# The input gate of the mLSTM branch as seven half-size products, query and key split for two token tiles at once, and a newly searched order

## The chip, the cores and the metric

The kernel runs on one core of a Trainium2 chip. The metric is the device time of one execution in microseconds; the kernel before took 1318.66 us (median of three runs, 1317.69 to 1319.36).

## The reference

Two layers of a decoder trunk, 512 tokens of width 1024, all in float32. One projection feeds two branches (differential attention and an mLSTM); the branches are gated, projected, merged by two sigmoid gates that are themselves slices of the projection, and projected again. Only the parts that matter here:

```python
def hybrid_layer(x, ...):
    h = rmsnorm(x, norm_g)
    proj = h @ w_in                                   # 512 x 1024 @ 1024 x 10256
    aq, ak, av, az, bqk, bv, bi, bf, bo, bz, ga, gb = jnp.split(proj, idx, axis=-1)
    q = rope(rmsnorm(two_map_heads(aq), q_norm_g), cos, sin)
    k = rope(rmsnorm(two_map_heads(ak), k_norm_g), cos, sin)
    ...
    ya = oa @ w_out_a                                 # attention branch
    ...
    yb = hb @ w_out_b                                 # mLSTM branch
    u = jax.nn.sigmoid(ga) * ya + jax.nn.sigmoid(gb) * yb
    return x + u @ w_o
```

`gb` is the gate on the mLSTM branch: `h` (512 x 1024) times a 1024 x 1024 slice of `w_in`.

## The kernel before

**Precision.** The matmuls take their operands as float32r. Each operand is split into a high part (a rounded copy, made by ScalarE) and a low part (the remainder, made by VectorE): `wh`, `wl` for weights, `hh`, `hl` for the normalised input. A product is three matmuls, high x high, high x low and low x high (`mm3`, L526).

**Pieces.** The projections are a list of pieces in the order of `TUNE["order"]`. Each piece brings one 128 x 1024 block of weights (512 KB), usually loaded by the SP queue into `wr` (two buffers), and split into `wh` and `wl`. Blocks named in `TUNE["dlo"]` are loaded by the POOL queue instead (`dh`), and their low part is formed by a copy and an accumulating load (`dl`). A feature piece (`feat_piece`: az, bqk, bo, bz, ga, gb, woa, wob; eight pieces each) makes 128 output features of all 512 tokens: 8 blocks of the inner dimension x 3 = 24 matmuls of 128 x 512 (128 columns of weights, 512 tokens moving). So `gb` costs 8 x 24 = 192 such matmuls in a layer. The gate's tanh goes to a small pool (`sgb`), and `wob_done` multiplies it in.

**Seven products.** `bv` and `wo` are not computed as eight half-size block products but as seven (`seven`, L904): left operand, right operand and output are each cut in 2 x 2 blocks, and sums of blocks are multiplied instead of blocks. The products are P1 to P7, each of two pieces. P1, P2 and P3 use weight blocks as they are; P5, P6 and P4 use a running sum `wws`, P7 a sum `wwt`. These sums are built by accumulating loads on the POOL queue or, for the steps in `TUNE["tdve"]`, by adds on VectorE (`load_sums` L1778, `prep_sums` L1794). The left operands P5, P6, P7 and P3 need are sums of blocks of `h`, called S1, S2, S3, S4 (`late_forms` L786), each a high and a low tile (`lhS`, `llS`). The products are summed in two PSUM chains of two tiles, X and Y, and one Z (`CHAIN`, L121).

**Queries and keys.** When a 128-token tile of a query-key column group has its norm and rotation, `qk_split` (L1077) transposes it on TensorE (four 128 x 128 transposes into one PSUM tile `qkt`), and ScalarE and VectorE split it into `qs`, `ks` and `kl`: per tile six copies and four subtractions on 64 partitions x 256 elements. `qkn` counts finished tiles; the attention scores of a head wait for them.

**Order.** All instructions are recorded first (`Recorder`, L128) and then put in order by a list scheduler with a table of costs and of biases (`schedule`, L298). Each engine then runs its instructions strictly in that order. Buffers come from pools; the largest, `qkp`, has 24 slots of 128 x 1024, shared by inputs, head outputs, operand sums, weight sums and `dh`/`dl`. A load that takes over a slot waits until the last reader of the slot's earlier tile is done, and what is queued behind it on SP or POOL waits too.

## Time and profile before

| what | value |
|---|---|
| median of 3 runs | 1318.66 us |
| the profiled execution's own time | 1318.76 us |
| its span on the page | 1317.0 us |
| VectorE busy | 1047.3 us (80%) |
| ScalarE busy | 941.6 us (71%) |
| GpSimd busy | 81.0 us (6%) |
| DMA, mean over the span | 128 GB/s |
| read from and written to HBM | 162.66 MB, 4.26 MB |

TensorE's rows are in the prediction. Each TensorE instruction has two rows in the profile, the weight load (PEld) and the matmul (PE). A matmul's recorded duration (some 390 ns at 128 x 512) is longer than the distance between two starts, since they are pipelined; what a matmul costs in a stream is the distance of the starts. "Busy" is the time covered by any record, so that what remains is idle time.

### The profile page before, as it was taken

To read this page: it belongs to the slowest core of one execution; us is meant where nothing else is said; L and a number is where in the kernel's file an instruction comes from. 1 tells how busy PE (TensorE), PEld (TensorE's weight loads), DVE (VectorE), ACT (ScalarE), POOL (GpSimd) and SP (SyncE) were. 2 spreads that over 40 slices of the span, in tenths; PEclk is the share of its full clock that TensorE was granted. 3 is DMA by queue.
4 is the path that set the end of the run, shared out by engine and by line. 5 is a ranking of instruction groups with operands and counts; after the bars stand their busy time and mean duration, and the time that the engine had idled before them with its cause. 6 is when DMAs were issued, how large, how long until landed. Compare 5 with 4: busy or idle time off the path is not lost.

```text
span 1317.0 us, 17544 instructions
## 1 busy us (share of the span) xinstructions
PE 1308.5 (99%) x6140; PEld 1084.6 (82%) x6140; DVE 1047.3 (80%) x1876; ACT 941.6 (71%) x1808; POOL 81.0 (6%) x104
## 2 busy tenths in 40 slices
PE   8999999999999999999999999999999999999998
PEld 6888888888888888888887888888888888888887
DVE  7899888897588788755887988888876788887466
ACT  6878789895367788743668787898944677887333
POOL 1000000000010000001101000000000101000000
PEclk9999999999999999999999999999999999999999
DMA  5222232233675465455954222322346655653656
GB/s 190 88 66 81 97 98 63 81 96 116 186 175 143 132 177 135 121 138 117 302 144 120 58 81 78 100 80 80 90 129 187 168 143 159 158 112 121 163 132 200
DMA packets 56744, 168.06 MB, mean 128 GB/s; under 512 B 6704, under 2 KB 13488, under 8 KB 56656
## 3 DMA queue, kind: packets, MB, share of 16 engines
q1 hardware_dynamic: 45712, 127.10, 30.7%
q0 software_dynamic: 10944, 39.85, 14.3%
q8 instruction: 48, 0.79, 0.2%
q14 instruction: 40, 0.33, 0.1%
HBM read 162.66 MB, written 4.26 MB: 127 GB/s over the span
## 4 chain that ended last, share of the span: by engine, by line
PE 96%; DVE 1%; DMA 1%; ACT 1%; issue 0%; SPq 0%; DVEq 0%; ACTq 0%
PE qk L474 13%; PE av L474 7%; PE az L474 7%; PE bo L474 7%; PE ga L474 7%; PE bqk L474 7%; PE bz L474 7%; PE woa L474 7%; PE gb L474 7%; PE wob L474 7%; PE wo_P L474 6%; PE bv_P L474 6%; PE sc L474 3%; PE num L474 2%; PE ms L474 2%; PE ut L474 1%
## 5 line engine op out<-in xcount | busy, mean ns | idle before, releaser
L474 ACT CAST wh<-wr 128x1024 fp32r<-128x1024 f32 x176 | 183.4, 1046 | 118.9 <-PE woa L474 27.9
L474 DVE TENSOR_TENSOR wl<-wr,wh 128x1024 fp32r<-128x1024 f32 (+1 forms) x178 | 212.6, 1196 | 54.3 <-ACT wh L474 53.0
L474 PE MATMUL qk<-wh,hh 128*128 128x512 f32 x240 | 88.6, 397 | 1.0 <-ACT hh L474 1.0
L474 PE MATMUL qk<-wl,hh 128*128 128x512 f32 x240 | 88.7, 399 | 0.3 <-DVE wl L474 0.3
L474 PE MATMUL qk<-wh,hl 128*128 128x512 f32 x240 | 87.3, 398 | 0.1
L473 ACT ACT_TABLE_LOAD x65 | 83.4, 1283 | 1.1
L474 ACT ACTIVATE p<-sc,mx,rq 128x128 f32<-128x128 f32 (+3 forms) x128 | 78.5, 618 | 6.3 <-DVE mx L474 5.5
L474 PE MATMUL woa<-oa,wh 128*128 128x512 f32 x224 | 71.7, 391 | 0.0
L474 PE MATMUL wob<-ob,wh 128*128 128x512 f32 x192 | 60.5, 389 | 0.0
L474 POOL DMA_DIRECT2D dl<-in_wp_dram x26 | 22.6, 871 | 532.7 <-ACT dl L474 406.3
L474 DVE TENSOR_REDUCE mx<-sc 128x2 f32<-128x256 f32 (+1 forms) x64 | 52.5, 820 | 0.8
L474 PEld LDWEIGHTS qk<-wh,hh 128*128 128x128 f32 x240 | 44.7, 188 | 9.8 <-ACT hh L474 1.3
L474 PEld LDWEIGHTS qk<-wl,hh 128*128 128x128 f32 x240 | 44.9, 188 | 9.5 <-DVE wl L474 0.9
L474 ACT CAST ks<-qkt 64x256 fp32r<-64x256 f32 x128 | 47.1, 368 | 7.4 <-DVE qs L474 5.7
L474 PEld LDWEIGHTS qk<-wh,hl 128*128 128x128 f32 x240 | 44.8, 188 | 8.9 <-DVE hl L474 0.4
L474 PEld LDWEIGHTS woa<-oa,wh 128*128 128x128 f32 x224 | 42.1, 188 | 8.7
L474 PE MATMUL az<-hl,wh 128*128 128x512 f32 x120 | 47.8, 399 | 0.0
L474 PE MATMUL az<-hh,wh 128*128 128x512 f32 x120 | 47.8, 399 | 0.0
L474 PE MATMUL az<-hh,wl 128*128 128x512 f32 x120 | 47.5, 397 | 0.0
L474 PE MATMUL av<-wl,hh 128*128 128x512 f32 x120 | 47.4, 395 | 0.0
L474 ACT CAST uh<-ut 128x128 fp32r<-128x128 f32 (+2 forms) x80 | 29.7, 372 | 24.7 <-PE ut L474 22.1
L474 PE MATMUL av<-wh,hl 128*128 128x512 f32 x120 | 47.2, 393 | 0.0
(378 smaller groups left out, 4013.1 us busy)
## 6 DMA issues: line engine op xcount, KB each, us to landing
wr<-in_wp_dram SPq DMA_DIRECT2D x174, 512.0 KB, 3.6
dh<-in_wp_dram POOLq DMA_DIRECT2D x26, 512.0 KB, 7.4
dl<-in_wp_dram POOLq DMA_DIRECT2D x26, 512.0 KB, 7.2
wws_wo<-in_wp_dram POOLq DMA_DIRECT2D x12, 512.0 KB, 5.9
dd<-rows SPq DMA_DIRECT2D x16, 256.0 KB, 4.9
wws_bv<-in_wp_dram POOLq DMA_DIRECT2D x8, 512.0 KB, 7.2
em<-rows SPq DMA_DIRECT2D x16, 256.0 KB, 6.8
dd<-rows SPq DMA_DIRECT2D x16, 192.0 KB, 5.4
```

The costliest lines, as they stand in the source:

```text
L473: self.tc.keep_in_program_order(self.nc.scalar.preload_act_table_set(self.SET_NAME[o["load"]]))
L474: self.tc.keep_in_program_order(getattr(o["e"], o["fn"])(*o["a"], **o["k"]))
```

## The change

Four things are changed together.

1. `gb` is made by `seven`, with the roles of the operands that the code calls FEAT7: weights are the stationary operand, half of the tokens (256) move. A product's piece has 4 feature blocks x 2 inner blocks x 3 = 24 matmuls of 128 x 256, so `gb` is 7 x 2 x 24 = 336 matmuls of 128 x 256 in a layer in place of 192 of 128 x 512. Its outputs (`gate_out`) are four tiles of the pool `s5`. S1 to S4 are formed once, for `bv`; because `gb` needs them again, `bv` writes them to DRAM (`h_spill`: eight 512 KB stores a layer) and `gb` reads them back (eight loads a layer).
2. `qk_split` waits for the second of two token tiles and works on both: two PSUM tiles (`qkt0` for queries, `qkt1` for keys), each of four transposes, and copies and subtractions of 64 x 512, half as many as before.
3. The scheduler's estimate of when a DMA lands is replaced (`land`), and some of its numbers are new.
4. `TUNE` is new: the order of the pieces, the biases, which norms are summed by a folded tile (`foldA`, `foldM`, `foldD`: folded, the sum over partitions takes one 128 x 512 matmul, unfolded two), which sums VectorE makes, and which blocks POOL loads.

The core of the diff:

```diff
 TUNE = {
     "order": (
-        ... bz6 bz7 gb3 wob3 gb4 gb2 wob2 wob4 gb0 gb5 wob0 wob5 gb1 gb6 wob1 gb7 wob6 wob7 wo.P5 ...
+        ... bo7 bo6 bz6 bz7 gb.P1 gb.P5 gb.P2 gb.P3 gb.P6 gb.P7 wob4 gb.P4 wob6 wob0 wob3 wob5 wob1 wob2 wob7 wo.P5 ...
     ),
-    "foldA": (1, 2, 3, 4, 5, 6, 7),
-    "foldM": (0, 1, 2, 3, 4, 5, 6, 7),
-    "foldD": (0, 1, 2, 3, 4, 5, 6, 7),
+    "foldA": (0, 2, 3, 4, 7),
+    "foldM": (1, 3, 4, 5),
+    "foldD": (0, 1, 2, 3, 4, 5, 6),
-    "tdve": {'bv': ('T2',), 'wo': ('T2', 'T3', 'T4')},
+    "tdve": {'bv': ('T1', 'T2', 'T4'), 'wo': ('T3',), 'gb': ('T2',)},
-    "lates": ('bv',),
+    "lates": ('bv', 'gb'),
...
         def qk_split(c, tt, rq):
-            def back():
-                pst = ps_tr.tile([P, 4, P], F32, tag="tr", name=f"qkt{l}_{c}_{tt}")
-                for g in range(4):
-                    T.transpose(pst[:, g, :], rq[:, g * P : (g + 1) * P], ident)
...
+            st[("rot", c, tt % 2)] = rq
+            if tt % 2 == 0:
+                return
+            rqs = [st[("rot", c, t)] for t in range(2)]
+            def back(side):
+                def f():
...
+                    pst = ps_tr.tile([P, 2, 2, P], F32, tag="tr", name=f"qkt{side}{l}_{c}_{tt}")
+                    for t in range(2):
+                        for g in range(2):
+                            T.transpose(pst[:, g, t, :], rqs[t][:, (2 * side + g) * P : (2 * side + g + 1) * P], ident)
...
+                    for r, (a, b) in enumerate(((L, H), (H, L))):
+                        t = st[("qs", c)][2 * side + r][:, :, ts]
+                        A.copy(t[a], src[a])
+                        if side:
+                            A.copy(t[b], src[a])
+                            t2_, o = st[("kl", c)][r][:, :, ts], a
+                        else:
+                            t2_, o = t, b
+                        V.tensor_tensor(t2_[o], src[a], t[a].bitcast(F32), ALU.subtract)
...
+            for side in range(2):
+                defer(TUNE["qkt"] + side, back(side))
```

How the order changes, at three places. In a row, the first number in a name is the layer; the tile written stands first, then what it is made from.

TensorE, layer 0, where `gb` begins before the change: a feature piece `gb0_3`, whose `wh87` and `wl87` are the high and low weights of one block, then `wob0_3`, and `gb0_4`.

```order
L474 MATMUL gb0_3_1011<-hh0_117,wl87_996 128x512
L474 MATMUL wob0_3_1029<-ob0_0_842,wh88_1003 128x512 x2
L474 MATMUL wob0_3_1029<-ob0_0_842,wl88_1004 128x512
L474 MATMUL wob0_3_1029<-ob0_1_866,wh88_1003 128x512 x2
L474 MATMUL wob0_3_1029<-ob0_1_866,wl88_1004 128x512
```

TensorE now, layer 0, inside `gb`: the tile `gb0_P5` is chain Y (for P5 and then P3), `gb0_P1` chain X (for P1, P6, P7, P4); `lhS20`/`llS20` and `lhS40`/`llS40` are the reloaded S2 and S4 of layer 0 (`lhS10`/`llS10`, S1, stand ahead); `num0_7` is the last mLSTM head.

```order
L498 MATMUL gb0_P5_0_1029<-lhS40_gb_1048,wh94_1056 128x256
L498 MATMUL gb0_P5_1_1030<-lhS40_gb_1048,wh94_1056 128x256
L498 MATMUL gb0_P5_0_1029<-llS40_gb_1049,wh94_1056 128x256
L498 MATMUL gb0_P5_1_1030<-llS40_gb_1049,wh94_1056 128x256
L498 MATMUL num0_7_1086<-sdl0_7_1046,bv0_1_0_767 128x512
L498 MATMUL gb0_P1_0_1021<-lhS20_gb_1060,wh95_1062 128x256
L498 MATMUL gb0_P1_1_1022<-lhS20_gb_1060,wh95_1062 128x256
```

The stretch of 128 x 512 matmuls, each on one block's weights, has become one of 128 x 256 with the reloaded sums as moving operand. The slot that `lhS20` is loaded into is that of `llS10`; between the last read of `llS10` and this first read of `lhS20` TensorE runs 53 matmuls, 44 of 128 x 256 and three each of 128 x 512, 128 x 384 and 128 x 128.

The SP queue, layer 0, at the end of the mLSTM heads, before: weight blocks `wr` and the last head's rows (`dd`, `em`).

```order
L474 DMA dd_7_1023<-rows 128x128
L474 DMA wr_1043<-in_wp_dram 128x1024
L474 DMA wr_1048<-in_wp_dram 128x1024
L474 DMA em_7_1024<-rows 128x512
L474 DMA wr_1053<-in_wp_dram 128x1024
```

The SP queue at the same place now:

```order
L498 DMA em_7_1001<-rows 128x512
L498 DMA lhS_gb<-dS1h_718 128x1024
L498 DMA llS_gb<-dS1l_719 128x1024
L498 DMA wwt_gb_1032<-in_wp_dram 128x1024
L498 DMA wr_1050<-in_wp_dram 128x1024
L498 DMA lhS_gb<-dS4h_729 128x1024
L498 DMA llS_gb<-dS4l_730 128x1024
L498 DMA wwt_gb_1051<-in_wp_dram 128x1024
L498 DMA wr_1055<-in_wp_dram 128x1024
L498 DMA lhS_gb<-dS2h_748 128x1024
L498 DMA llS_gb<-dS2l_749 128x1024
L498 DMA wr_1076<-in_wp_dram 128x1024
```

Between the weight blocks stand the reloads of S1, S4 and S2 and the first blocks of the sums; a weight block that is queued behind a reload waits for the reload's slot.

ScalarE, layer 0, where the second query-key group is split, before (`ks`, `qs` from the transposed tile `qkt0_1_0` of the first 128 tokens):

```order
L474 CAST ks00_1_280<-qkt0_1_0_314 64x2x128
L474 ACTIVATE sq0_1_3_300,qss0_1_2_298<-qk0_1_3_248 128x64 x4
L474 CAST qs10_1_279<-qkt0_1_0_314 64x2x128
L474 ACTIVATE qy0_1_3_302<-qss0_1_2_298,eps64_104 128x16
L474 ACTIVATE qy0_1_3_302<-qy0_1_3_302 128x16
```

ScalarE now (`qkt00_1_1` holds the queries and `qkt10_1_1` the keys of the first 256 tokens):

```order
L498 CAST qs10_1_279<-qkt00_1_1_319 64x2x256
L498 ACTIVATE qy0_1_3_301<-qy0_1_3_301 128x16
L498 CAST wh17_324<-wr17_321 128x1024
L498 ACTIVATE rot0_1_2_294<-rot0_1_2_294,rq0_1_284 128x64 x4
L498 CAST ks00_1_280<-qkt10_1_1_320 64x2x256 x2
```

The copies cover twice the tokens, and each stands once for two tiles.

More of the change, by code (lines that the diff above doesn't have):

```diff
@@ L37 @@
 TUNE = {
+    "land": (0.4, 300.0, 885.0, 2560.0, 3650.0),
     "order": (
[4 rows of a table removed]
[4 rows of a table added]
     ),
     "qkt": 5,
-    "gct": 15,
-    "gls": 1,
-    "glf": 0,
-    "attn": (0, 1, 6, 10, 10, 13, 15, 16, 19, 26),
+    "gct": 11,
+    "gls": 2,
+    "glf": 1,
+    "attn": (0, 8, 8, 12, 14, 14, 15, 16, 20, 27),
     "a0": 24,
     "ap": 18,
-    "a4": 18,
-    "ml": (6, 7, 12, 17, 19, 31),
+    "a4": 20,
+    "ml": (8, 8, 21, 21, 29, 41),
     "ahead": 3,
-    "lc": 4,
-    "slack": 2311.1,
+    "lc": 10,
+    "slack": 366.3,
     "margin": 0.0,
-    "pemargin": 117.1,
-    "wait": 228.9,
+    "pemargin": 141.5,
+    "wait": 162.2,
     "swpen": 141896579.9,
-    "smargin": 231.5,
+    "smargin": 781.4,
     "pwait": 0.0,
-    "wdiff": 7859.5,
+    "wdiff": 6612.9,
     "wsp": 4,
-    "kact": (0, 1, 2),
-    "qsq": (3,),
-    "foldA": (1, 2, 3, 4, 5, 6, 7),
-    "foldM": (0, 1, 2, 3, 4, 5, 6, 7),
-    "foldD": (0, 1, 2, 3, 4, 5, 6, 7),
+    "kact": (1, 2),
+    "qsq": (1, 3),
+    "foldA": (0, 2, 3, 4, 7),
+    "foldM": (1, 3, 4, 5),
+    "foldD": (0, 1, 2, 3, 4, 5, 6),
     "warm": 18,
@@ L72 @@
     "acl": 7,
-    "gateA": 6,
+    "gateA": 2,
     "gateM": 1,
-    "actp": (0, 1, 2, 3),
-    "m0": 224,
-    "mp": 18,
-    "m4": 8,
+    "actp": (2, 3),
+    "m0": 228,
+    "mp": 13,
+    "m4": 3,
     "slots": 24,
-    "hfd": 4,
+    "hfd": 20,
     "tset": (0, 18),
@@ L83 @@
     "pmask": 0,
-    "dlo": ('av0.3', 'az0', 'az6', 'bo1', 'bo4', 'bo6', 'bo7', 'bqk3', 'bz4', 'ga3', 'gb2', 'qk1.2', 'qk1.3', 'woa4', 'wob1', 'wob5'),
-    "dla": 5,
+    "dlo": ('av1.1', 'az0', 'az2', 'az3', 'az6', 'bo1', 'bo4', 'bo6', 'bo7', 'bqk3', 'bz3', 'ga3', 'ga5', 'gb0', 'gb1', 'qk0.3', 'qk1.2', 'qk2.0', 'woa0', 'woa4', 'woa6', 'wob1', 'wob5'),
+    "dla": 6,
     "groups": (),
@@ L92 @@
-    "drain": 105.8,
-    "group": 570.6,
-    "lates": ('bv',),
-    "risk": 118.2,
-    "late": 395.7,
[3 rows of a table added]
+    "drain": 137.0,
+    "group": 984.3,
+    "lates": ('bv', 'gb'),
+    "risk": 2827822086695.3,
+    "late": 10125509.6,
 }
@@ L291, in rate, with land @@
         if o["k"].get("accum_op") is not None:
-            return 150.0
-        return 175.0 if src.tensor.name.startswith("rows") else 250.0 if src.space != DRAM else 360.0
+            return 204.0
+        if o["eng"] == "POOL":
+            return 514.0
+        if src.space == DRAM and src.tensor.name.startswith("rows"):
+            return 138.0
+        return 316.0 if src.space == DRAM and math.prod(list(o["a"][0].shape)) >= 131072 else 310.0
+    def land(self, o, go, queue):
+        z = int(o["eng"] == "POOL")
+        size = 4.0
+        for x in list(o["a"][0].shape):
+            size *= x
+        w = size / self.rate(o)
+        share, g0, g1, f0, f1 = TUNE["land"]
+        own = 1.0 - share if z else share
+        t = max(go + (g1 if z else g0), queue[z])
+        r = queue[1 - z] - t
+        if r <= 0:
+            fin = t + w
+        elif w / own <= r / (1.0 - own):
+            d = w / own
+            fin = t + d
+            queue[1 - z] = fin + (r - d * (1.0 - own))
+        else:
+            d = r / (1.0 - own)
+            queue[1 - z] = t + d
+            fin = t + d + (w - d * own)
+        queue[z] = fin
+        return fin + (f1 if z else f0)
     LAT = {("ACT", "DVE"): 131, ("ACT", "PE"): 262, ("ACT", "ACT"): 153, ("DVE", "ACT"): 130, ("DVE", "PE"): 240, ("DVE", "DVE"): 127,
@@ L343, in schedule @@
         end = [0.0] * n
-        dma = 0.0
+        queue = [0.0, 0.0]
         table = 6
@@ L426, in schedule @@
             if o["fn"] == "dma_start":
-                size = 4.0
-                for x in list(o["a"][0].shape):
-                    size *= x
-                go = s + c if e == "POOL" else s
-                dma = max(dma, go) + size / self.rate(o)
-                end[i] = max(dma, go) + (5500.0 if e == "POOL" else 5000.0 if o["a"][1].tensor.name.startswith("rows") else 3000.0)
+                end[i] = self.land(o, s + c if e == "POOL" else s, queue)
             for t in o["tiles"]:
@@ L1003, in f @@
             def f():
-                if ("qd", c, tt) not in st or tt and st.get(("qkn", c), 0) < tt or not tt and not room(6):
+                if tt % 2 == 0:
+                    return
+                if ("qd", c, tt) not in st or tt > 1 and st.get(("qkn", c), 0) < tt - 1 or tt == 1 and not room(6):
                     return False
-                if not tt:
+                if tt == 1:
                     qk_take(c)
-                rq = t2(f"rl{l}_{c}_{tt}")
-                SY.dma_start(rq, st["qd", c, tt])
-                qk_split(c, tt, rq)
+                for t in (tt - 1, tt):
+                    rq = t2(f"rl{l}_{c}_{t}")
+                    SY.dma_start(rq, st["qd", c, t])
+                    qk_split(c, t, rq)
             return f
@@ L1058, in qk_done @@
             V.tensor_tensor(rqv, y, t, ALU.mult)
+            back = [st[("rot", c, t % 2)] for t in (tt - 1, tt)]
             for t in (tt - 1, tt):
-                qk_back(c, t, st[("rot", c, t % 2)])
+                qk_back(c, t, back[t % 2])
         def qk_back(c, tt, rq):
@@ L1095, in qk_split @@
-            defer(TUNE["qkt"], back)
+            st[("rot", c, tt % 2)] = rq
+            if tt % 2 == 0:
+                return
+            rqs = [st[("rot", c, t)] for t in range(2)]
+            def back(side):
+                def f():
+                    if side and ("qkq", c, tt) not in st:
+                        return False
+                    pst = ps_tr.tile([P, 2, 2, P], F32, tag="tr", name=f"qkt{side}{l}_{c}_{tt}")
+                    for t in range(2):
+                        for g in range(2):
+                            T.transpose(pst[:, g, t, :], rqs[t][:, (2 * side + g) * P : (2 * side + g + 1) * P], ident)
+                    ts = slice((tt - 1) * P, (tt + 1) * P)
+                    L, H = slice(0, 64), slice(64, 128)
+                    src = pst.rearrange("p g t k -> p g (t k)")
+                    for r, (a, b) in enumerate(((L, H), (H, L))):
[4 more added lines that the diff above has]
+                            t2_, o = st[("kl", c)][r][:, :, ts], a
+                        else:
+                            t2_, o = t, b
+                        V.tensor_tensor(t2_[o], src[a], t[a].bitcast(F32), ALU.subtract)
+                    if side:
+                        st[("qkn", c)] = tt + 1
+                    else:
+                        st["qkq", c, tt] = 1
+                return f
```

13 lines of the change are left out of this document (removed), and 10 rows, old and new, of the table TUNE.

## The prediction

> **What bounds the kernel now.** First the page's head, which has TensorE (PE) covered almost throughout, then the busy time by stages, which says where the rest lies, then the chain of waits.
>
> ```profile
> span 1317.0 us, 17544 instructions
> PE 1308.5 (99%) x6140; PEld 1084.6 (82%) x6140; DVE 1047.3 (80%) x1876; ACT 941.6 (71%) x1808; POOL 81.0 (6%) x104
> ```
>
> ```profile
> core 0: us, PE busy (x) PEld busy (x) DVE busy (x) ACT busy (x) POOL busy (x), PEclk, DMA share, GB/s
> 0.00:30.00 30.00, 26.58 (x120) 20.43 (x121) 22.49 (x70) 18.07 (x34) 4.95 (x9) 1.00 0.60 208
> 330.00:370.00 40.00, 40.00 (x178) 33.10 (x177) 25.20 (x27) 18.19 (x22) 4.31 (x5) 1.00 0.70 193
> ...
> 622.00:655.00 33.00, 33.00 (x147) 27.00 (x146) 29.20 (x38) 19.90 (x28) 4.19 (x5) 1.00 0.94 302
> 700.00:716.00 16.00, 14.99 (x74) 12.32 (x73) 12.43 (x27) 11.35 (x29) 0.00 (x0) 1.00 0.57 183
> ...
> 1290.00:1317.00 27.00, 22.95 (x101) 18.45 (x99) 17.11 (x21) 6.24 (x6) 1.73 (x2) 0.97 0.52 155
> ```
>
> PE is idle for 8.5 us. The first 30 us hold 3.42 of it (inputs on their way), the last 27 us 4.05 (the output leaving), 700 to 716 us 1.01: 8.48 together. Between start and tail there is one hole of 1 us, where a transpose waited for the split of the keys:
>
> ```profile
> PE ut L474 <- DVE kl L474: 1.0, 1, 1.0
> ```
>
> So the time is the sum of the distances between matmul starts, at a granted clock of 1.00. A new order can win back that hole and little else; what it can lose has no such bound. VectorE and ScalarE matter only where they make PE wait.
>
> What a matmul costs in a stream, by its width: in the chain of waits 45 of 128 x 512 in a row; in two stretches of the timeline of PE runs of four 128 x 256, with the start in the first column (the third row of each is what follows).
>
> ```profile
> 568.74 10.20 PE gb L474 x45
> ```
>
> ```profile
> 266.65 0.39 PE L474 MATMUL sc<-ks,qs 128*128 128x256 f32 x2
> 266.88 0.40 PE L474 MATMUL sc<-kl,qs 128*128 128x256 f32 x2
> 267.12 0.80 PE L474 MATMUL av<-uh,av 128*128 128x512 f32 x3
> ...
> 284.81 0.40 PE L474 MATMUL sc<-ks,qs 128*128 128x256 f32 x2
> 285.05 0.41 PE L474 MATMUL sc<-kl,qs 128*128 128x256 f32 x2
> 285.29 0.38 PE L474 MATMUL ut<-ct,p 128*128 128x128 f32 x2
> ```
>
> The wide one costs 10.20 / 45 = 226.7 ns; eight narrow ones took 0.47 + 0.48 us, 118.75 ns each. Two narrow ones cost 237.5 ns, 5% more than the wide one they replace. That eats part of what seven products save over eight.
>
> **The change part by part.**
>
> *The gate's matmuls.* The 2 x 192 that go stand in six groups of the trace, three like the first row and, for the blocks that POOL loads, three like the second:
>
> ```profile
> L474 PE MATMUL gb<-hh,wh 128*128 128x512 f32 x112 | 43.6, 390 | 0.0
> ...
> L474 PE MATMUL gb<-hl,dh 128*128 128x512 f32 x16 | 6.2, 390 | 0.0
> ```
>
> They are 3 x 112 + 3 x 16 = 384, at 226.7 ns 87.05 us. In come 2 x 336 = 672 of 128 x 256, at 118.75 ns 79.80 us. The trace has these only in runs of up to four, while the gate makes long streams. The nearest rows bound the price: half a wide one, 113.3 ns (76.2 us), below, and the dearer run, 120 ns (80.6 us), above. I take the mean of both runs, since a run's later starts are no further apart than its first. The break-even comes out of the sum below and lies close, at 124.8 ns.
>
> *The Trainium skill on this term.* By "TensorE: Matmul & The Clock Gate", section "Back-to-back issue gap", an isolated gap is N/2.4 + 2.5 ns, 109.2 and 215.8 ns; with these two the whole sum below would be an estimate of 6.5 us saved. The rows above have both widths some 10 ns higher, so the measurement decides.
>
> *Unfolded norms.* The new tables unfold 4 attention norms, 8 mLSTM norms and 2 denominators over both layers: 14 more matmuls of 128 x 512, 3.17 us on PE.
>
> *The sum on PE.* 87.05 - 79.80 - 3.17 = 4.08 us less; with the bounds 3.2 to 7.7 us. Transposes, scores and the other projections are as many as before, only moved.
>
> *Queries and keys in pairs.* ScalarE and VectorE, by these groups; the last two give the price of 64 x 512:
>
> ```profile
> L474 ACT CAST ks<-qkt 64x256 fp32r<-64x256 f32 x128 | 47.1, 368 | 7.4 <-DVE qs L474 5.7
> L474 ACT CAST qs<-qkt 64x256 fp32r<-64x256 f32 x64 | 23.4, 365 | 9.6 <-DVE kl L474 7.7 <-PE qkt L474 0.8
> L474 DVE TENSOR_TENSOR qs<-qkt,qs 64x256 fp32r<-64x256 f32 x64 | 27.0, 422 | 7.9 <-ACT qs L474 5.9
> L474 DVE TENSOR_TENSOR kl<-qkt,ks 64x256 fp32r<-64x256 f32 x64 | 26.8, 419 | 11.6 <-ACT ks L474 10.5
> L474 ACT CAST mk<-cv 64x512 fp32r<-64x512 f32 x16 | 9.7, 617 | 0.2
> L474 DVE TENSOR_TENSOR mk<-cv,mk 64x512 fp32r<-64x512 f32 x16 | 11.0, 686 | 1.3 <-ACT mk L474 0.9
> ```
>
> ScalarE goes from 70.5 to 96 x 0.617 = 59.2 us, VectorE from 53.8 to 64 x 0.686 = 43.9 us: 11 and 10 us less on engines that PE did not wait for, except in the 1 us hole. What the pairing costs is time until the first tile's scores may start. PE has other products queued then, so I put it at nothing; without that cover a hole like the old one costs 1 us. For the order as a whole I take nothing, between -1 us (hole closed) and +2 us (two such holes).
>
> *What the gate adds elsewhere.* VectorE gets eight weight sums of 128 x 1024 (four for `bv`, four for `gb`) and twelve adds of 128 x 512, over both layers about 8 x 1.2 + 12 x 0.69 = 18 us by this group and the last one above:
>
> ```profile
> L474 DVE TENSOR_TENSOR wl<-wr,wh 128x1024 fp32r<-128x1024 f32 (+1 forms) x178 | 212.6, 1196 | 54.3 <-ACT wh L474 53.0
> ```
>
> They lie beside PE, as does the split of a piece (1.2 us of VectorE in the 2.85 us of its 24 matmuls): from 622 to 655 us VectorE is busy for 29.20 of 33 us, and PE does not wait. Without that cover each sum would cost PE its 1.2 us. The DMAs are the point. In the gate's stage in after's order the SP queue issues 18 transfers of 512 KB (six weight blocks, four first blocks of sums, eight reloads of S1 to S4) and 1.8 MB of rows for two heads, the POOL queue eight of 512 KB. Their price by the queues' rows:
>
> ```profile
> q1 hardware_dynamic: 45712, 127.10, 30.7%
> q0 software_dynamic: 10944, 39.85, 14.3%
> ```
>
> The SP queue: 0.307 x 1317 / 127.10 = 3.18 us of all 16 engines a MB, 1.67 us for 512 KB (0.524 MB). POOL: 0.143 x 1317 / 39.85 = 4.73, 2.48 us. The stage needs 18 x 1.67 + 1.8 x 3.18 + 8 x 2.48 = 55.6 us of DMA. Its PE work is 344 x 0.11875 + 39 x 0.2267 = 49.7 us and 12 small matmuls below 0.2 us each: about 51 us. So DMA is full unless some 5 us or more of it is issued ahead of the stage, which the lookahead (two raw blocks, seven pieces for sums) allows. With the share at 0.94 between 622 and 655 us PE was busy for 33.00 of 33 us, and at 0.70 in `bv`, the seven-product stage that most resembles this one, for 40.00 of 40. I take no wait, and keep the other end as rivals. The eight stores of S1 to S4 fall into `bv`, which loses two weight-sum loads on SP and two on POOL a layer: up from 0.70 by (6 x 1.67 - 2 x 2.48) / 40 = 0.13, still below 0.94.
>
> *The forecast.* The profiled execution took 1318.76 us (span 1317.0), 0.1 us over the median of the runs shown. 1318.76 - 4.1 = **1314.7 us**.
>
> **The rivals.**
>
> *S2 comes late.* `lhS20` takes over a slot of S1. From the last read there to its first read PE runs 53 matmuls, 44 narrow ones (5.2 us), three wide (0.7 us) and six others (about 0.85): 6.7 us for issue and landing. The load's two prices, in the windows of `bv` and of 622 to 655 us:
>
> ```profile
> wr<-in_wp_dram SPq DMA_DIRECT2D x8, 512.0 KB, 3.6
> ```
>
> ```profile
> wr<-in_wp_dram SPq DMA_DIRECT2D x6, 512.0 KB, 8.5
> ```
>
> At 3.6 us it lands in time. At 8.5 plus about 0.6 to see the release and issue, PE waits 2.4 us; behind the waiting matmul stand the rest of P3 and all of P6, and behind the load on SP only what is read later (`wob4`'s block, S3's pair). That is 4.8 us in two layers, **1319.5 us**, no change. For: nearly full DMA engines. Against: S4's pair has 11 us and should have drained by then. 20%. Holes of the new order adding up to the same, 7%.
>
> *DMA binds the whole gate.* If nothing is issued ahead, the stage takes 55.6 / 0.94 = 59 us in place of 51: 8 us a layer, **1331 us**, slower. It turns slower from 3.4 us a layer. For: the sum above, and slots that come free late. Against: the 33.00 of 33 us at a share of 0.94. 10%.
>
> *Weight loads show.* A narrow matmul brings as many weights as a wide one. If a long stream were paced by the load's record of 0.19 us (its rows below, the timeline of PEld in the first stretch), 672 x (188 - 118.75) = 47 us would be added: **1361 us**.
>
> ```profile
> 266.77 0.30 PEld L474 LDWEIGHTS sc<-kl,qs 128*128 128x128 f32 x2
> 267.00 0.54 PEld L474 LDWEIGHTS av<-uh,av 128*128 128x128 f32 x3
> ```
>
> But two loads fit in 0.30 us, overlapping, and the starts stay 118 ns apart. 3%. The same page of the Trainium skill, section "Part 3: Packing small matmuls", says that weight loads overlap with running matmuls only when they target another row group; by that rule each of the 302 added matmuls would show its load. The trace does not agree: the loads here use all 128 rows and lie inside the distance of the starts.
>
> *It saves more.* Narrow matmuls at 113.3 ns or the hole closed: 1310 to 1312.5 us. 8%.
>
> **How the numbers follow.** Forecast 52%, more 8%, no change 27% (S2 20, holes 7), slower 13% (DMA 10, loads 3). A difference of 0.2%, 2.6 us, is about what a measurement of this kernel can tell from no change. Faster, below 1316.0: 0.60; same: 0.27; slower, above 1321.3: 0.13. The range takes in the saving's bounds and S2 coming late: 1310 to 1321 us, leaving out the 13%.
>
> **What would show it.** In the profile after: runs of `gb_P` matmuls with starts 118 to 120 ns apart (at 124.8 the saving is gone); PE busy without a hole over the gate's 51 us, and a DMA share there of 0.9 or more; no wait of `gb_P` on a DMA of `lhS` (S2's rival is an idle time of PE ahead of the first matmul that reads it); fewer and longer copies from `qkt`; idle time at start and tail as before. The forecast is wrong if the sum of PE's idle time grows by more than 2 us, or if a narrow matmul in a long stream costs another price than in a run of four.

## The result, and the profile after

The changed kernel is slower, not faster:

| kernel | median | lowest to highest | runs | ratio to before (95%) |
|---|---|---|---|---|
| before, beside it | 1318.61 us | 1317.69 to 1319.36 | 9 | |
| changed | 1325.23 us | 1321.33 to 1332.94 | 9 | 1.0062 (1.0047 to 1.0077) |

That is 6.6 us more, where the forecast had 4.0 less and the range ended at 1321. The second thing to see is the spread: 11.6 us, where the kernel before has 1.7. The profiled execution took 1332.73 us and is one of the longest of the nine, so a second profile was taken later (below); one profile of a kernel with such a spread is not its median. All medians leave out one execution, of e10, which took 1438.05 us at a granted clock (the share of TensorE's full clock that the profile shows as granted) of 0.851.

The head of the page, and TensorE's waits in that first profile (in total, times, longest):

```profile
span 1331.0 us, 18309 instructions
PE 1314.2 (99%) x6442; PEld 1101.2 (83%) x6442; DVE 1062.0 (80%) x1856; ACT 915.4 (69%) x1770; POOL 96.1 (7%) x124
```

```profile
PE gb_P L498 <- DMA llS_gb<-dS3l: 5.1, 2, 2.9
PE num L498 <- DVE ms_b L498: 2.2, 1, 2.2
```

PE is idle for 16.8 us, 8.3 more than before. The last line is a head of the mLSTM branch in layer 1, the first is the gate: once in each layer its product P7 waits for the low tile of S3, reloaded from DRAM. S2, which the prediction named as the rival, is not in the list. By stages, with start, `bv`, the gate in layer 0, 622 to 655 us and the gate in layer 1:

```profile
0.00:30.00 30.00, 26.15 (x107) 20.20 (x108) 19.60 (x50) 16.56 (x30) 4.64 (x9) 0.94 0.58 208
330.00:370.00 40.00, 40.00 (x178) 33.13 (x177) 23.77 (x23) 17.24 (x20) 1.73 (x2) 1.00 0.69 210
535.00:600.00 65.00, 62.74 (x434) 58.74 (x433) 45.56 (x59) 46.35 (x63) 8.02 (x10) 0.97 0.84 240
622.00:655.00 33.00, 32.58 (x143) 26.35 (x142) 30.94 (x46) 17.87 (x24) 4.08 (x5) 1.00 0.72 206
1190.00:1255.00 65.00, 62.15 (x430) 58.16 (x429) 46.98 (x61) 48.18 (x66) 8.02 (x10) 0.97 0.83 228
```

The gate loses 2.3 and 2.9 us to idle time, and its granted clock is 0.97, where it was 1.00. The hole between 700 and 716 us is gone (16.00 of 16 busy). In the second profile of the same kernel, of an execution of 1323.28 us, the wait on S3 stands first again:

```profile
PE gb_P L498 <- DMA llS_gb<-dS3l: 3.3, 2, 2.5
PE warm L498 <- DVE ml L498: 1.6, 1, 1.6
PE num L498 <- DVE ms_b L498: 1.0, 1, 1.0
```

(The `warm` line is the start, as before; `num` is another head here, in layer 0 at 526 us.) So the wait on S3 belongs to the kernel, not to one execution. Part of what separates 1332.7 from 1323.3 us shows in the clock behind it. After the wait in layer 0, in the first profile and in the second:

```profile
572.78 0.38 PE L498 MATMUL gb_P<-llS_gb,wh 128*128 128x256 f32 x1 [2.26 <-DMA llS_gb<-dS3l]
...
574.61 0.63 PE L498 MATMUL gb_P<-lhS_gb,wh 128*128 128x256 f32 x2
575.04 0.63 PE L498 MATMUL gb_P<-llS_gb,wh 128*128 128x256 f32 x2
575.47 0.63 PE L498 MATMUL gb_P<-lhS_gb,wl 128*128 128x256 f32 x2
```

```profile
572.45 0.39 PE L498 MATMUL gb_P<-llS_gb,wh 128*128 128x256 f32 x1 [2.48 <-DMA llS_gb<-dS3l]
...
573.87 0.40 PE L498 MATMUL gb_P<-lhS_gb,wh 128*128 128x256 f32 x2
574.11 0.40 PE L498 MATMUL gb_P<-llS_gb,wh 128*128 128x256 f32 x2
574.35 0.40 PE L498 MATMUL gb_P<-lhS_gb,wl 128*128 128x256 f32 x2
```

In the second the pairs start 0.24 us apart, 120 ns a matmul. In the first, from some 0.9 us behind the end of the wait, the matmuls are slow, and the pairs start 0.43 us apart, 214 ns each: the clock is at half, and the windows say so (from 574 to 577 us in the first, from 572 to 575 in the second):

```profile
574.00:577.00 3.00, 3.00 (x16) 3.00 (x16) 0.00 (x0) 0.00 (x0) 0.00 (x0) 0.50 1.08 416
```

```profile
572.00:575.00 3.00, 2.55 (x21) 2.55 (x22) 0.96 (x2) 0.40 (x1) 0.00 (x0) 1.00 1.10 385
```

PE is fully busy in the first and makes 16 matmuls; the second makes 21 in the same 3 us, with 0.45 us idle. Sixteen slow matmuls cost 16 x 94 ns = 1.5 us, which no list of waits shows. Both profiles have the same order of matmuls, so they can be set against each other start by start. Of the 9.5 us by which the first falls behind, 4.8 arise at the two waits on S3 with the slow matmuls behind them, 1.4 in the first 30 us (where the first profile also has 3.4 us at half clock), 1.2 at the two heads and 2.1 in `wo` of layer 0.

### The profile page after: what moved, and what is told of

The parts are those of the page before. It is cut to its first block, busy times and chain, and to the rows that moved or that the text cites. A ratio compares the mean times of both kernels' runs of the same rounds, so it can differ in the third digit from the quotient of the medians.

```text
span 1331.0 us, 18309 instructions
## 1 busy us (share of the span) xinstructions
PE 1314.2 (99%) x6442; PEld 1101.2 (83%) x6442; DVE 1062.0 (80%) x1856; ACT 915.4 (69%) x1770; POOL 96.1 (7%) x124
## 4 chain that ended last, share of the span: by engine, by line
PE 91%; DMA 5%; DVE 2%; ACT 1%; issue 1%; SPq 0%; DVEq 0%; ACTq 0%
PE qk L498 13%; PE av L498 9%; PE ga L498 7%; PE bo L498 7%; PE bqk L498 7%; PE woa L498 7%; PE wob L498 7%; PE az L498 6%; PE bz L498 6%; PE gb_P L498 5%; PE wo_P L498 4%; PE bv_P L498 4%; PE sc L498 3%; PE num L498 2%; DMA llS_gb<-dS3l 2%; PE ms L498 1%
## 5 line engine op out<-in xcount | busy, mean ns | idle before, releaser
L498 ACT CAST wh<-wr 128x1024 fp32r<-128x1024 f32 x166 | 172.4, 1043 | 115.1 <-DMA wr<-in_wp_dram 30.2
L498 DVE TENSOR_TENSOR wl<-wr,wh 128x1024 fp32r<-128x1024 f32 (+1 forms) x168 | 199.9, 1195 | 34.9 <-ACT wh L498 32.2
L498 PE MATMUL qk<-wl,hh 128*128 128x512 f32 x224 | 80.8, 397 | 0.4 <-DVE wl L498 0.4
L498 PE MATMUL qk<-wh,hh 128*128 128x512 f32 x224 | 79.4, 397 | 1.0 <-ACT wh L498 1.0
L498 PE MATMUL woa<-oa,wh 128*128 128x512 f32 x192 | 62.8, 390 | 0.0
L498 PE MATMUL av<-wh,hh 128*128 128x512 f32 x120 | 47.4, 401 | 0.0
L498 PE MATMUL ga<-hh,wh 128*128 128x512 f32 x112 | 44.7, 399 | 0.0
L498 PE MATMUL ga<-hl,wh 128*128 128x512 f32 x112 | 44.2, 395 | 0.0
L498 PE MATMUL ga<-hh,wl 128*128 128x512 f32 x112 | 44.1, 394 | 0.0
L498 PE MATMUL bz<-hh,wh 128*128 128x512 f32 x112 | 43.8, 391 | 0.0
```

The source lines that it names most:

```text
L498: self.tc.keep_in_program_order(getattr(o["e"], o["fn"])(*o["a"], **o["k"]))
```

## The experiments

The theory after the first of these profiles (A): the reload of S3 comes late in both layers, and the rest is what follows from it, above all the half clock. The rivals: the matmuls of 128 x 256 cost more in long streams than in runs of four (B); the new order, the pairs or the unfolded norms cost it (C). The runs, all against the kernel before on the same chip:

| label | what | median | ratio (95%) |
|---|---|---|---|
| e1 | no stores and reloads of S, scheduled anew | 1321.21 | 1.0021 (1.0012 to 1.0031) |
| e2 | the gate as eight products, all else of the change | 1334.30 | 1.0116 (1.0099 to 1.0133) |
| e3 | before, with the pairs alone | 1319.94 | 1.0010 (1.0001 to 1.0020) |
| e4 | S formed again for the gate | 1369.12 | 1.0381 (1.0366 to 1.0397) |
| e5 | changed order, no stores and reloads of S | 1319.04 | 1.0003 (0.9993 to 1.0012) |
| e6 | as e5, and no accumulating loads for the gate | 1316.87 | 0.9985 (0.9976 to 0.9994) |
| e7 | changed order, reloads kept, no accumulating loads | 1320.15 | 1.0011 (1.0001 to 1.0021) |
| e8 | changed order, only S3's stores and reloads out | 1321.68 | 1.0021 (1.0012 to 1.0031) |
| e9 | the changed kernel again | 1323.28 | 1.0056 (1.0028 to 1.0084) |
| e10 | changed order, reloads out, stores kept | 1322.46 | 1.0029 (1.0017 to 1.0040) |
| e11 | S as one full tile, less traffic, new order | 1320.83 | 1.0020 (1.0011 to 1.0029) |
| e12 | S as in the change, new order | 1321.17 | 1.0020 (1.0011 to 1.0029) |
| e13 | as e10, two accumulating loads less in layer 1 | 1320.84 | 1.0015 (1.0006 to 1.0025) |
| e14 | as e10, the stores of layer 1 out | 1320.14 | 1.0013 (1.0003 to 1.0022) |

**e1: no S through DRAM, scheduled anew.**

```diff
-                    if n != formed[-1]:
-                        h_spill(op)
...
-                    for w, x in zip("hl", both):
-                        SY.dma_start(x.bitcast(F32), st[op, w])
...
-                                bh, bl = lhs(LEFT[prod], 2 * a + k, None)
+                                bh, bl = lhs({"S1": "A11", "S2": "A00", "S3": "A10", "S4": "A01"}.get(LEFT[prod], LEFT[prod]), 2 * a + k, None)
```

> The gate's seven products read blocks of h in place of the sums S1 to S4 (the sums of blocks are left out of the gate's left operands, so the output is another one); the 16 stores and 16 reloads of S are gone, the matmuls are as many and as wide. Theory A (PE waits for the reload of S3, and the clock drops behind the wait): the two waits of 2.9 and about 3 us and the slow matmuls behind them go, 1325.2 - 2 x 5 = 1315 us (1313 to 1317), PE idle below 11 us, clock at or above 0.999. Rival B (the narrow matmuls in long streams are the cost): 1323 us or more, since the same 672 matmuls run. Rival C (the new order and the pairs of query and key are the cost): 1321 us or more.

1321.21 us: 4.0 below the changed kernel, with the same 672 narrow matmuls, so B is out as the main cause. The waits on S3 are gone. But 1315 was expected, and the median sits on C's bound. One wait is left, the `num` of a head in layer 1, now 2.6 us and with eleven slow matmuls behind it. Since removing the transfers let the scheduler choose anew, this run mixes two things; e5 repeats it with the order held.

**e2: the gate as eight products, with the rest of the change.**

```diff
-        "bqk1 ... bz6 bz7 gb.P1 gb.P5 gb.P2 gb.P3 gb.P6 gb.P7 wob4 gb.P4 wob6 wob0 wob3 wob5 wob1 wob2 wob7 ..."
+        "bqk1 ... bz6 bz7 gb3 wob3 gb4 gb2 wob2 wob4 gb0 gb5 wob0 wob5 gb1 gb6 wob1 gb7 wob6 wob7 ..."
-    "lates": ('bv', 'gb'),
+    "lates": ('bv',),
```

> The changed kernel with the gate on the mLSTM branch as eight products again, all its other numbers, the pairs and the unfolded norms kept (no S is stored or reloaded). Theory A: the gate's loss of 10 us goes and its saving of 7 us too; what stays are 3.2 us of unfolded norms and the start, 1320 to 1323 us. Rival C: 1325 us or more. Rival B does not tell it from A. If it comes below 1317 us, the order and the pairs alone gain, and all of the loss is the gate's.

1334.30 us: above the 1320 to 1323 us of A, and in the range that was given to C (1325 us or more). But its waits are others than those of the changed kernel:

```profile
PE msp_b L498 <- DVE fo_b L498: 4.6, 2, 2.3
PE ms L498 <- DVE dd L498: 1.7, 2, 0.9
```

PE waits for VectorE at the ends of mLSTM heads, where numbers searched for one list of pieces now order another. So the run does not tell the parts of the change apart: the order that it measures is not the changed kernel's order, and C is left to e5 and e6.

**e3: the pairs alone**, put into the kernel before.

```diff
-            def back():
-                pst = ps_tr.tile([P, 4, P], F32, tag="tr", name=f"qkt{l}_{c}_{tt}")
...
+            if tt % 2 == 0:
+                return
+            rqs = [st[("rot", c, t)] for t in range(2)]
...
+            for side in range(2):
+                defer(TUNE["qkt"] + side, back(side))
```

> The kernel before with the splitting of queries and keys for two tiles at a time, nothing else. Theory A and my prediction's step (the pairing lies off the path): 1318.6 us, within 1.5. Rival C: 3 us or more above, with waits of ut or sc on the copies from the transposes.

1319.94 us, 1.2 above before (0.1 to 2.6 by the interval) and within the 1.5 us expected. The pairs may cost something, but they are not the main cause.

**e4: S formed again** for the gate, by VectorE and ScalarE.

```diff
-                    if n != formed[-1]:
-                        h_spill(op)
...
-        if n in TUNE["lates"] and (prod, a) == ("P1", 0) and "lf" not in layers[l][3]:
+        if n in TUNE["lates"] and (prod, a) == ("P1", 0) and not layers[l][3].get("lf"):
```

> The changed kernel with S1 to S4 formed a second time for the gate by ScalarE and VectorE; the 16 stores and 16 reloads are gone, the result is the same. Theory A: no wait on a DMA of S, but PE may wait for the sums, which need an add of 128x1024 and a split each, about 4 x 3 us of VectorE a layer beside the gate's 29 of 33 us: 1314 to 1320 us. Rival B or C: 1322 us or more. If it comes above 1325 us with PE waiting for VectorE in the gate, VectorE has taken the place of the DMAs.

1369.12 us. VectorE and ScalarE have taken the place of the DMAs, and more. PE now waits for them at the last heads and at the sums themselves:

```profile
PE ms L498 <- DVE dd L498: 7.1, 8, 1.3
PE msp_b L498 <- DVE fo_b L498: 6.3, 2, 3.2
PE gb_P L498 <- ACT lhS_gb L498: 4.6, 4, 1.9
```

and the granted clock of the whole execution falls to 0.986.

**e5 and e6: the order held.** Here every instruction is issued in the changed kernel's order, and transfers are left out of it at the last moment. The gate's matmuls read blocks of h in place of the sums (`alt`). e6 leaves out the accumulating loads of `gb`'s weight sums as well. The diff is that of e6; e5 lacks the part of the condition from the second `or` on.

```diff
         for i in order:
             o = self.ops[i]
...
-            self.tc.keep_in_program_order(getattr(o["e"], o["fn"])(*o["a"], **o["k"]))
+            a = o["a"]
+            if o["fn"] == "dma_start":
+                d, s = a[0].tensor.name, a[1].tensor.name
+                if d.startswith("dS") or s.startswith("dS") or o["k"].get("accum_op") is not None and "_gb_" in d:
+                    continue
+            if "alt" in o:
+                a = (a[0], a[1], o["alt"])
+            self.tc.keep_in_program_order(getattr(o["e"], o["fn"])(*a, **o["k"]))
```

> Every instruction in the changed kernel's order; only the 16 stores and 16 reloads of S1 to S4 are taken out, and the gate's matmuls read blocks of h in place of S (the sums of blocks are left out of the gate's left operands). Unlike the first run without reloads nothing else moves. Theory A (the late reload of S3, and the half clock behind the wait): the two waits on S3 and the slow matmuls behind them go, some 4.2 us a layer; 1325.2 - 8.5 = 1316.7 us (1315 to 1319). Rival (DMA as a whole is too full in this order, by the weight sums as well): the wait of num on the last head's rows in layer 1 (2.2 us) stays, 1319 us or more. Rival C (the order itself costs it, not DMA): 1323 us or more.

> As the run before, and the gate's 12 accumulating loads by the POOL queue are taken out too (the sums of weight blocks lack these terms). Order and matmuls stay. If the accumulating loads delay the last head's rows in layer 1, the wait of num on ms_b goes: 3 us less than the run before, 1313 to 1316 us, which would be the forecast's term for the matmuls alone. If those rows are late for another reason (queued behind other loads on SP), within 1 us of the run before.

e5: 1319.04 us, 6.2 less than the changed kernel, for 32 transfers that compute nothing. That is all but 0.4 us of the loss against before. It is no proof that S3's wait is all of it: that was A's 1316.7, and the result lies on the border to the rival, "DMA as a whole too full". e6: 1316.87 us, 2.2 less again, and with the transfers out there is nothing left in the gate or in the heads (waits longer than 1 us: only the start). The gate's two windows in e5 and in e6:

```profile
535.00:600.00 65.00, 64.88 (x450) 60.41 (x449) 47.74 (x62) 47.74 (x65) 8.02 (x10) 1.00 0.72 182
1190.00:1255.00 65.00, 65.00 (x432) 59.62 (x431) 48.18 (x61) 45.88 (x62) 8.01 (x10) 1.00 0.70 177
```

```profile
535.00:600.00 65.00, 65.00 (x444) 60.38 (x443) 47.70 (x60) 47.07 (x63) 4.57 (x6) 1.00 0.52 148
1190.00:1255.00 65.00, 65.00 (x426) 59.49 (x425) 48.36 (x62) 43.71 (x57) 5.45 (x7) 1.00 0.55 154
```

PE is covered throughout, at a clock of 1.00. e6 is the seven-product gate with nothing late, and it is 1.8 us faster than before (0.8 to 3.2 us by the interval above). So rival C falls as well: apart from the matmuls of the unfolded norms, which are counted in the sum on PE below, the order and the pairs together cost little.

**e7: reloads kept, the gate's twelve accumulating loads out** (the sums lack these terms). The edit is the condition of e6 without its first two terms, and no `alt`.

> The changed kernel in its order with all reloads, without the gate's 12 accumulating loads (the sums of weight blocks lack these terms). If the reload of S3 is late because the accumulating loads share the DMA engines with it (two of them were issued within 4 us of it), it lands in 4 to 6 us and the waits on S3 go: 1316 to 1319 us. If the reloads are late by themselves (issued late, when the slot comes free, and eight in a row on SP), the waits stay: 1323 us or more.

1320.15 us, 5.1 less than the changed kernel, though all 32 transfers of S stand in it. The reload of S3 in layer 0, in the changed kernel and in e7:

```profile
lhS_gb<-dS3h SPq DMA_DIRECT2D x1, 512.0 KB, 8.5
```

```profile
lhS_gb<-dS3h SPq DMA_DIRECT2D x1, 512.0 KB, 3.7
```

What PE waits for is the low tile, which follows on the same queue. Its landing shows in layer 1, again in the changed kernel and in e7:

```profile
llS_gb<-dS3l SPq DMA_DIRECT2D x1, 512.0 KB, 12.6
```

```profile
llS_gb<-dS3l SPq DMA_DIRECT2D x1, 512.0 KB, 5.2
```

It lands at 1231.78 us in the changed kernel, and the matmul that waits for it starts at 1231.83. Issued at the same place of the order, both tiles land early when POOL's accumulating loads do not run beside them, and the waits on S3 are gone. From e6, where both are out, the accumulating loads alone add 2.2 us (e5) and S alone 3.3 us (e7), but the two together 8.4 us (the changed kernel): some 2.9 us are due to their running side by side. The size is uncertain, since the interval of the changed kernel alone is 2 us wide to either side; that the reload lands late beside the accumulating loads does not hang on it.

**e8: only S3 out.** `alt` for S3 alone (P7 reads a block of h in its place), and the condition `"dS3"`.

> The changed kernel in its order; only S3's stores and reloads (4 and 4) are taken out, and the product P7 reads a block of h in place of S3. Theory A: the waits on S3 were 2.4 and 3.0 us with 1.5 and 1.6 us of half clock behind them, 8.5 us together: 1316.7 us, as without all four. If the wait moves to S2 or S4 or to the weight sum behind it, 1320 us or more.

1321.68 us, 3.5 less. The gate of layer 0 is then without a hole:

```profile
535.00:600.00 65.00, 65.00 (x448) 60.45 (x447) 47.73 (x61) 46.80 (x63) 8.03 (x10) 1.00 0.82 230
```

at a DMA share of 0.82, hardly less than the 0.84 at which it waited. So the share is not the number that decided; which transfer is late decided. But A's 8.5 us is not there. It was taken from the long first profile; in the second, the two waits on S3 lengthen the distance between starts by 2.6 and 1.0 us, which is about what e8 gives back. The other 2.6 us, from e8 to e5, go with the transfers of S1, S2 and S4.

**e9: the changed kernel again.** The unaltered kernel.

> The changed kernel once more, unaltered, for a second profile: its runs spread from 1321.3 to 1332.9 us and the first profile fell on 1332.7. If the waits on S3 in both layers are its own (theory A), they stand in this profile too, with the half clock behind them where they reach some 2.4 us, and a run near 1325 us has shorter ones. If they were an accident of that execution, they are missing and the time over the kernel before lies elsewhere.

1323.28 us (1321.68 to 1332.83 in five runs). Its waits are shown above. Of the fourteen executions of this kernel, the five with a granted clock of 0.999 or 1.0 took 1321.3 to 1323.3 us, the nine with 0.995 to 0.997 took 1324.2 to 1332.9. So the long executions are those in which the clock dropped; where it dropped is known for the profiled one alone. Set against e6, whose order is the same, the second profile is 6.7 us behind. At S3 it loses 2.8 and 1.1 us, in the two stages of `bv` 0.7 and 0.8, at the head in layer 0 1.1 and in the first 30 us 0.7; elsewhere it wins 0.4 back.

**e10: the stores without the reloads.** The condition of e5 without `d.startswith("dS")`.

> The changed kernel in its order; the 16 stores of S stay, only the 16 reloads are taken out (the gate's products read blocks of h in place of S). If the reloads alone do the harm, as without both: 1319.0 us, within 1. If the stores in bv cost too (their share of the DMA engines there was put at 0.83, no wait), 1320 us or more, with PE waiting in bv.

1322.46 us, 3.4 above e5: the stores cost as well. In this profile neither `bv` nor the gate has a wait of 0.3 us on anything; what is left is the head in layer 1, at 3.8 us. That head's rows are four loads behind two 512 KB loads of `wws_gb` on SP, and POOL issues two accumulating loads of `wws_gb` beside them. From issue to landing, the last of the four took, in the changed kernel, in its second profile, in e6 and in e10:

```profile
dd<-rows SPq DMA_DIRECT2D x1, 64.0 KB, 9.6
```

```profile
dd<-rows SPq DMA_DIRECT2D x1, 64.0 KB, 7.3
```

```profile
dd<-rows SPq DMA_DIRECT2D x1, 64.0 KB, 7.4
```

```profile
dd<-rows SPq DMA_DIRECT2D x1, 64.0 KB, 11.5
```

PE's wait there was 2.2, 0, 0 and 3.8 us; in e5 8.3 and 0.9, in e7 9.0 and 1.4, in e1 9.9 and 2.6. In every one of these profiles with a wait, PE's matmul starts 1.33 us after that landing, so the rows are what it waits for. They are the second place where the change made PE wait. But each of these figures is of one execution, and the two profiles of the changed kernel differ by 2.2 us, so the differences between the kernels are not shown by them. Nor are the accumulating loads needed for the wait: e7 has none. Two questions stayed: whether the accumulating loads beside the rows delay them, and where the stores come in.

**e11 and e12: the same products with less traffic or more time.** In both, VectorE makes the gate's last weight sum, P2 comes behind P6, and the norms are folded in eight more places, so that TensorE makes eight matmuls fewer; the biases and some numbers of the scheduler are new. e11 also sends S through DRAM once, unsplit:

```diff
-    "foldA": (0, 2, 3, 4, 7),
+    "foldA": (0, 1, 2, 3, 4, 5, 6, 7),
-    "foldD": (0, 1, 2, 3, 4, 5, 6),
+    "foldD": (0, 1, 2, 3, 4, 5, 6, 7),
-    "tdve": {'bv': ('T1', 'T2', 'T4'), 'wo': ('T3',), 'gb': ('T2',)},
+    "tdve": {'bv': ('T1', 'T2', 'T4'), 'wo': ('T3',), 'gb': ('T2','T4')},
...
-                    split(*st[op], st["lf"].pop(op))
-                    give(1)
+                    full = st["lf"].pop(op)
                     if n != formed[-1]:
-                        h_spill(op)
+                        d = st[op, "f"] = dram.tile([P, D], F32, name=f"d{op}f{l}")
+                        SY.dma_start(d, full.rearrange("p k t -> p (k t)"))
+                    split(*st[op], full)
+                    give(1)
                 else:
-                    for w, x in zip("hl", both):
-                        SY.dma_start(x.bitcast(F32), st[op, w])
+                    SY.dma_start(both[1].bitcast(F32), st[op, "f"])
+                    A.copy(both[0], both[1].bitcast(F32))
+                    V.tensor_tensor(both[1], both[1].bitcast(F32), both[0].bitcast(F32), ALU.subtract)
```

> The gate as seven products with less traffic, result unchanged: each S goes to DRAM as one full tile before it is split and is split again after the reload (8 stores and 8 reloads in all in place of 16 and 16), the gate's last weight sum is added by VectorE (8 accumulating loads in place of 12) with P2 behind P6, six of the fourteen norms are folded again (1.4 us of TensorE less), and the table of biases is new. Theory A with its second half (reloads and accumulating loads are harmless apart and late together): no wait on S or on a sum above 1 us, granted clock 0.999 or more, 1314 to 1318 us. If the splits after the reload stand in the way, PE waits for ScalarE's copy to lhS or VectorE's llS and the time is 1320 us or more.

> As the run before, but S in high and low tiles through DRAM as in the changed kernel (16 stores, 16 reloads); 8 accumulating loads, P2 behind P6, the same norms folded, a table of biases of its own. It tells what the reloads alone still cost where four accumulating loads are gone and the order leaves them more time: 1316 to 1320 us if the two queues were the cause, with the wait on S3 below 1 us; 1323 us or more if reloads issued when slots come free are late in any order.

1320.83 us (1319.78 to 1323.11) and 1321.17 us (1319.85 to 1321.75): some 4 us below the changed kernel, and its spread is gone; all 22 executions show a clock of 0.998 or more. The waits on S3 are gone as well; the longest on a reload is, in e12,

```profile
PE gb_P L498 <- DMA llS_gb<-dS2l: 0.6, 1, 0.6
```

But both times lie above the 1318 and 1320 us that were expected, and above the kernel before. In e11 the waits are many and short, and they are on VectorE and ScalarE now:

```profile
PE ms L498 <- DVE dd L498: 1.5, 3, 0.5
PE gb_P L498 <- ACT sbo L498: 0.7, 1, 0.7
PE gb_P L498 <- ACT p_gb L498: 0.5, 1, 0.5
```

They are not what the rival named: the longest on a split behind a reload (`llS_gb`) is 0.2 us. The late transfers can be ordered away; the seven-product gate still does not pay in these two orders, and why it stays above before is open. Of the kernels that leave nothing out, none was faster than the one before.

**e13 and e14: the rows and the stores.** e13 takes two accumulating loads out of e10, e14 the stores of layer 1.

```diff
+                first = o["k"].get("accum_op") is not None and d.startswith("wws1_gb") and d not in seen
+                if first:
+                    seen.add(d)
-                if s.startswith("dS"):
+                if s.startswith("dS") or first:
                     continue
```

```diff
-                if s.startswith("dS"):
+                if s.startswith("dS") or d.startswith("dS") and d[4] == "1":
                     continue
```

> The kernel of e10 (changed order, stores kept, reloads out, the gate's products on blocks of h), and in layer 1 alone the first accumulating load into each of the two sums wws_gb is taken out too (the sums of weight blocks lack these terms): the two that POOL issues beside the rows of head 6. Theory (those rows, behind the sums' loads, make num wait): that head's wait, 3.8 us in e10's profile with about 1.2 us of slow matmuls behind it, goes, and the last of its rows lands in 7.5 us or less: 1318 to 1319.5 us. If the accumulating loads beside the rows have no part in it (the loads of wws_gb on SP ahead of the rows alone, or the stores in another way): within 1 us of e10's 1322.7.

> The kernel of e10 with the stores of layer 0 alone (eight in place of sixteen; reloads out in both layers). e10 lost 3.7 us to e5 by the stores, and its profile shows it in layer 1. If the stores of layer 1 do it, 1319 us as in e5; if a state that the stores of layer 0 leave does it, 1322 us; if each layer bears its share, about 1321 us.

e13: 1320.84 us, 1.6 below e10. The wait of that head is 1.5 us and did not go, the rows took 9.7 us to land. The expectation failed, then: the two accumulating loads bear part of the wait at most, and even that is not shown, since the intervals of e13 and e10 overlap. The loads of `wws_gb` ahead of the rows on the same queue do not make the rest alone, for they stand there in e6 too, without a wait. e14: 1320.14 us, 2.3 below e10 and 1.1 above e5. That speaks for the stores of layer 1, but the intervals of e14 overlap with both. In e14 the only wait of `bv` is in layer 0, where the stores are,

```profile
PE bv_P L505 <- ACT wh L505: 0.4, 1, 0.4
```

and the changed kernel has it in both layers (0.7 us, two times), e5 in neither. But e10 has stores in both layers and no such wait, so that the stores make it is not shown. How stores of layer 1 could delay a landing more than 100 us later stays open as well.

## Why the prediction was wrong, step by step

- **What bounds the kernel** (the sum of matmul starts, and "what it can lose has no such bound"): right. The loss is idle time and slow matmuls, on top of a sum that did fall.
- **The price of the narrow matmul**, 118.75 ns: 120 in the long streams (0.24 us a pair in the second profile), the upper bound. Over 672 matmuls that is 0.84 us, and 1.6 with the joints between pieces (below). The weight loads did not show (the 3% rival).
- **The sum on PE**, 4.08 us: in e6, where nothing is late, the distances of all starts, without the waits, add up to about 1.6 us less than before. The 370 wide ones fewer take 83.6 us with them, the 672 narrow ones bring 81.4 (121 ns with the joints between pieces, where the stream changes its width), and the smaller shapes, as many as before, 0.6. Sign and mechanism were right, the size was some 2.5 us too large. The kernel e6 as a whole gained 1.8 us.
- **The pairs of queries and keys** at nothing: right within 1.5 us (e3, 1.2). ScalarE's copies from `qkt` took 37.2 + 18.6 = 55.8 us (59.2 forecast), VectorE's subtractions 44.1 (43.9).
- **The order** between -1 and +2 us: the hole of 1 us went, and in the first profile the first 30 us lost 0.4 us more to idle time than before. In e6 the waits come to 0.4 us less than before.
- **"I take no wait"** for the gate's DMAs: this is the step that failed. The demand was estimated well (55.6 us for 51 us of PE; in the second profile, from 535 to 590 us, the DMA engines were busy for 0.86 x 55 = 47 us, and four of the gate's transfers, two sums' loads on POOL and S1's pair, had been issued ahead of it). The error was the cover. TensorE's idle time grew by 8.3 us in the first profile and by 4.1 in the second, where the forecast had it unchanged. That PE was busy for 33.00 of 33 us at a share of 0.94 says that a stage can run at such a share, not that this one does. Here eight reloads are issued when a slot comes free and are read some 10 us later. What decides is the slack of each such load against its landing beside the other transfers. S3's low tile in layer 1 had 9.8 us from its issue to the moment when PE came to it. It landed after 12.6 and 10.5 us in the two profiles of the changed kernel, late, and after 5.2 us in e7, without the accumulating loads and in time. In e8, without S3, the gate of layer 0 has no hole at a share of 0.82.
- **The rival "S2 comes late"** had the mechanism, with landing 8.5 us, and the wrong tile. S2's slack was put at 6.7 us, and it landed in 6.1 us in the first profile; S3, which the next product reads, was not looked at. Its load was issued at 560.4 us, and POOL issued four loads within the next 5 us. And the rival's price, 2.4 us a layer, left out the half clock behind it (1.5 us), which made 4 us of it in the first profile; in the second there was none.
- **Not seen at all**: the rows of a head in layer 1, late in one of the two profiles of the changed kernel. The prediction counted the sums' loads in the gate's stage; four of them are issued in the stage ahead of it, beside these rows. With neither these accumulating loads nor S (e6) the rows are in time; which of them delays the rows by how much stays open.
- **DMA binds the whole gate** (1331 us) did not happen: in both profiles the gate has one hole a layer, not a lack throughout.

Together, from the forecast to the median: 2.2 us mainly from the smaller saving (1314.7 to e6's 1316.9), 2.2 us from the accumulating loads (e6 to e5), 6.2 us from S through DRAM on top of them (e5 to 1325.2). Of the 6.2, 3.5 go with S3 alone (e8). The last two figures carry the uncertainty of the changed kernel's median, some 2 us.

## What to carry to other kernels

When a change trades TensorE work for transfers, do not weigh the stage's DMA share against its length: list each transfer that cannot be issued ahead, with its slack from the release of its slot to its first read, and set the slack against the landing time that the same queue pair shows when the other queue is busy, not when it is idle. Look one stage ahead as well, since loads that run ahead of their stage then stand beside those that another stage needs. And price a wait of 2.4 us or more on TensorE at its length, with some 1.5 us of slow matmuls behind it as the worse case.

## What the runs showed of the hardware

- **Half clock after a wait.** Six waits of PE that added 2.4 to 3.9 us to the distance between two starts stand in these profiles behind a stretch at full clock. Behind four of them (2.4 and 3.0 us in the first profile, 2.8 in e1, 3.9 in e10) 11 to 17 matmuls ran at about half clock, 1.4 to 1.6 us more; behind two (2.4 in the first profile, 2.6 in the second) none did. In the four, the clock fell 3.1 to 3.6 us after PE had gone idle. No wait below 2 us was followed by such a stretch. (e2 and e4, where waits follow close on one another, are not counted, nor are the first 20 us, where five profiles, those of e2, e5, e7, e8 and the first of the changed kernel, have one such stretch behind waits of about 1 us.) The slow stretch is some 16 x 214 ns = 3.4 us long. The Trainium skill, "TensorE: Matmul & The Clock Gate", section "Part 1: The HAM clock gate (the "warmup" mystery)", says that the clock falls to half after one idle window of about 3.4 us, and that the windows run freely and do not start anew with the kernel. The length of the slow stretch agrees with such a window, and free-running windows would explain that two waits of like length end differently; no run here tested that. The trace does not agree that the wait must last 3.4 us: 2.4 was enough.
- **Two queues.** The reloads of S2 and S3, 512 KB each on SP, landed in 3.7 to 5.2 us in the gate without accumulating loads (e7) and in 4.4 to 12.6 us beside them (both profiles of the changed kernel); those took 8 to 11 us themselves where they ran beside S3. S1's pair took 9 to 12 us in all three, so accumulating loads are not the only thing that delays a load. The Trainium skill, "DMA: Bandwidth & Descriptors", section "Queues, rings and completion order", says that each DMA engine goes round its queues packet by packet; e7 is in line with it, 8.5 against 3.7 us for the same load; that the queues take turns by packets no run here shows.
- **128 x 256 in a long stream** goes at 120 ns, 240 a pair, 6% over the 226.7 ns of one of 128 x 512.
